# Forgetting attention inside a decoder block: one reduction over two neighbouring PSUM banks, query tiles in falling order, the causal mask written into the loaded row

## The chip, the cores and the metric

The kernel runs on one core of one Trainium2 chip. The metric is the device time of one execution in microseconds (us). The engines are TensorE (PE, matmul; PEld is its weight load), VectorE (DVE), ScalarE (ACT), GpSimd (POOL) and SyncE (SP, which issues most of the DMAs). An SBUF or PSUM tile has 128 partitions; a PSUM bank holds 512 fp32 values in each.

## The reference

One decoder block on 1024 tokens of width 1024. The part that matters here is forgetting attention: 8 heads of dimension 64, causal, with a decay that is summed up over the keys and subtracted from the logits, so that it acts as a row of 1024 numbers, one for each key, of each head.

```python
c = jnp.cumsum(log_f, axis=1)
logits = jnp.einsum('bqhd,bkhd->bhqk', qi, k).astype(jnp.float32) * scale
logits = logits + ci[..., None] - c_k
causal = pi[:, None] >= key_pos[None, :]
logits = jnp.where(causal, logits, -jnp.inf)
p = jax.nn.softmax(logits, axis=-1).astype(v.dtype)
return jnp.einsum('bhqk,bkhd->bqhd', p, v)
...
mix = jnp.concatenate([att, sg], axis=-1)
h = h + mix @ w_out[layer]
h = h + conv_ffn(rmsnorm(h, norm_ffn_g[layer]), w_up[layer], conv_w[layer], conv_b[layer], w_down[layer])
```

The other half of the width (`sg`) is a chunked spatial gating. Behind both stand the output projection, a norm, and a gated MLP with a short convolution.

## The kernel before

The kernel goes through stages: the input projections and the gating (to about 226 us in the trace), attention (226 to 391 us), the output projection with the second norm (to about 440), the up projection with the convolution (to about 858) and the down projection (to the end, 1075). Precision beyond that of the fast matmul comes from splitting an operand into a high and a low half, so that most products are made of two or three matmuls. In attention, ACT casts the high half and DVE computes the low one.

The order of instructions on each engine in attention is not written out by hand. The scheduler places them, with a few extra order edges (`after`). An engine carries out its own instructions in that order, so one that waits holds up everything behind it on its engine.

**One head (`att_head`, L752 to 831).** SP issues five loads: the queries `A` (L756), the keys `B` (L757), the head's row of decay sums, broadcast to all partitions, `ck` (L758), and the keys' other half `B2` in two pieces (L759, L760). `A` and `B` share a tile `x1`, `ck` and `B2` share a tile `x2`; each has two buffers, so that a head's loads can start when the head before the last has finished with the buffer. Then come four query tiles `i`, in the order 0, 1, 2, 3, each with two query blocks `j` = 2i and 2i+1 of 128 queries. Block `j` needs the first n = (j+1) x 128 keys. For each block:

- POOL copies the last one to four 128-column pieces of `ck` into the block's tile `t`, setting what the causal mask forbids to a large number (L776);
- PE computes the logits in one or two PSUM banks of 512 keys (tag `s`, four buffers), two matmuls each (L783, L784);
- DVE reduces each bank in one instruction (L786): the row is combined with the logits, written to `t`, and the minimum over the keys comes out. For blocks 4 to 7 there are two of these, and the second starts from the first one's minimum `mn`. In the trace each shows as two records, the reduction and the read of its accumulator;
- ACT takes the exponential of the whole block, with the minimum as bias (L789).

Then, for each pair of 128 keys, PE transposes the weights into a PSUM bank (L812), ACT casts the high half `pt` (L813), DVE computes the low half (L814), and PE multiplies with the values (L822; "PV" below). After an odd tile the two tiles' result in `po` is evacuated by ACT (L828) and DVE (L829).

**Around the heads.** `row_tail` (L724) turns the row sums of a finished head into reciprocals (DVE, L729), transposes them and sends them through DRAM back to 64 partitions (L734, L735). It stands in the tile 0 of the next head. `pair_end` (L738) scales and splits the result of two heads; it runs on POOL for the first three pairs (L744, L747, L750), in tile 2 of heads 2, 4 and 6, and on DVE for the last. `wo_load` copies and splits the output projection's weights on POOL (L873, L874): for the first two tiles they are ordered behind masks of head 5, for the other two behind the last of head 7.

**Fillers.** The gating half's share of the output projection (`sg_out`, L833 to 856) is cut into 16 units of 12 matmuls, which are handed out between query tiles by the list `FILLS`, one or two at a time: they stand in heads 0 to 2, and none is left from head 3 on.

**After attention.** The output projection's matmuls (`wmm`, L963 to 965) take four parts of the width, k = 0 to 3, each from one pair of heads. In the profile before, 17 of the 72 of k = 0 to 2 stand between the last matmuls of attention. The results are added to the residual at L973.

PSUM has eight banks: four with tag `b` (transposes, results, fillers) and four with tag `s` (logits), in the pool `psa`, which lives for the whole kernel.

Of the kernel before, what the change touches and what calls it, by code (L numbers as in the profile page):

```python
# [64 lines left out]
def block_kernel(ctx: ExitStack, tc: tile.TileContext, xT, xtok, wuv, wv, wqk, wf, cpk, bfv,  # L65
# [12 lines left out]
    psa = ctx.enter_context(tc.tile_pool(name="psa", bufs=4, space=bass.MemoryType.PSUM))  # L78
# [673 lines left out]
    def att_head(h, order=(0, 1, 2, 3)):  # L752
# [13 lines left out]
        for i in order:  # L766
# [3 lines left out]
            for jj in range(2):  # L770
# [4 lines left out]
                c0 = (j // 4) * 512  # L775
                sel = pool.affine_select(out=t[:, c0:n], in_=ck[:, c0:n], pattern=[[-1, n - c0]], compare_op=ALU.is_ge,  # L776
                                   fill=BIG, base=j * P - c0, channel_multiplier=1)
                mn = sml.tile([P, 2], F32, tag="mn", name=nm("mn"))
                lo_ = lim[:, 0:1]
                for c in range(0, n, 512):  # L780
                    e = min(n, c + 512)
                    ps = sbank()
                    pe.matmul(ps[:, 0:e - c], A[:, qs], B[:, c:e], start=True, stop=False)  # L783
                    pe.matmul(ps[:, 0:e - c], A[:, qs], B2[:, c:e], start=False, stop=True)  # L784
                    m = mn[:, c // 512:c // 512 + 1]
                    dve.tensor_tensor_reduce(out=t[:, c:e], in0=ps[:, 0:e - c], in1=(t if c == c0 else ck)[:, c:e], scale=1.0,  # L786
                                             scalar=lo_, op0=ALU.add, op1=ALU.min, accum_out=m)
                    lo_ = m
                ex = act.activation(t, t, AF.Exp, bias=lo_, scale=-1.0, accum_out=rs[:, j:j + 1])  # L789
                exs.append(ex)  # L790
            sels[h].append(sel)
            if h == 7 and i == 3:
                wo_load((2, 3))
                row_tail(7, None)
            if h > 0 and i == 0:
                row_tail(h - 1, ex)
            if h in (2, 4, 6) and i == 2:
                pair_end(p - 1, sel)
            for _ in range(FILL[4 * h + list(order).index(i)]):
                next(filler, None)  # L800
            if i % 2 == 0:
                po = bank()
# [21 lines left out]
            if i % 2 == 1:  # L824
# [65 lines left out]
    early.release()  # L890
    upl = tc.alloc_tile_pool(name="upl", bufs=1, reuse_waits="tile")
# [560 lines left out]
```

## Time and profile before

| | us |
|---|---|
| median of 3 runs | 1077.31 (1076.47 to 1077.58) |
| the profiled execution's own time | 1076.71 |
| its span in the trace | 1075.0 |
| attention, about 226 to 391 | 165 |
| in it: PE busy | 162.4 |
| in it: DVE busy | 122.9 |
| in it: ACT busy | 105.7 |
| in it: POOL busy | 59.5 |

The busy times of attention are those of the window from 226 to 391 us. In the rows of a timeline the first number is the start in us from the beginning of the span, the second the duration, then come engine, line, operation, what is written and what is read, the shape, and in brackets how long the engine sat idle before and what released it; "x2" joins two neighbours of one kind. A row of a grouped view gives, behind the bar, busy time in us and the mean duration in ns, then the idle time ahead of the group and its releasers.

### The profile page before, as it was taken

To read this page: it belongs to the slowest core of one execution; us is meant where nothing else is said; L and a number is where in the kernel's file an instruction comes from. 1 tells how busy PE (TensorE), PEld (TensorE's weight loads), DVE (VectorE), ACT (ScalarE), POOL (GpSimd) and SP (SyncE) were. 2 spreads that over 40 slices of the span, in tenths; PEclk is the share of its full clock that TensorE was granted. 3 is DMA by queue.
4 is the path that set the end of the run, shared out by engine and by line. 5 is a ranking of instruction groups with operands and counts; after the bars stand their busy time and mean duration, and the time that the engine had idled before them with its cause. 6 is when DMAs were issued, how large, how long until landed. Compare 5 with 4: busy or idle time off the path is not lost.

```text
span 1075.0 us, 14470 instructions
## 1 busy us (share of the span) xinstructions
PE 1062.7 (99%) x5013; PEld 876.6 (82%) x5013; DVE 892.4 (83%) x1363; ACT 568.0 (53%) x984; POOL 249.5 (23%) x223
## 2 busy tenths in 40 slices
PE   9999999999999999999999999999999999999997
PEld 7888788787888888878888888888888888888886
DVE  5985798775689969999899999989988776898774
ACT  6666644554468855764444444444444444454653
POOL 0002134233046541054333333333322000000000
PEclk9999999999999999999999999999999999999999
DMA  9242267937557445132244513222331899433442
GB/s 345 90 140 96 74 156 218 278 118 224 188 166 207 129 137 185 72 117 98 98 137 164 170 69 127 98 98 98 108 118 45 289 326 317 125 95 97 141 125 96
DMA packets 66297, 160.80 MB, mean 150 GB/s; under 512 B 7976, under 2 KB 8240, under 8 KB 66224
## 3 DMA queue, kind: packets, MB, share of 16 engines
q1 hardware_dynamic: 65792, 159.32, 45.4%
q8 instruction: 39, 0.64, 0.2%
q10 hardware_dynamic: 432, 0.57, 0.1%
q14 instruction: 34, 0.28, 0.1%
HBM read 117.06 MB, written 42.80 MB: 149 GB/s over the span
## 4 chain that ended last, share of the span: by engine, by line
PE 77%; ACT 2%; DVE 2%; issue 1%; POOL 0%; DMA 0%; DVEq 0%; ACTq 0%
PE k L1306 19%; PE qa L1054 11%; PE qc L1054 11%; PE qd L1054 11%; PE qb L1054 5%; PE pb L822 3%; PE pb L812 2%; PE ps L257 2%; PE pf L852 1%; PE pf L853 1%; PE pf L851 1%; PE ps L783 1%; PE ps L784 1%; PE pb L964 1%; PE pb L963 1%; PE pb L965 1%
## 5 line engine op out<-in xcount | busy, mean ns | idle before, releaser
L1306 PE MATMUL k<-whb,wha 128*128 128x512 f32 x924 | 209.7, 389 | 0.0
L1306 PEld LDWEIGHTS k<-whb,wha 128*128 128x128 f32 x924 | 173.3, 188 | 36.2 <-DVE wha L159 0.2
L1054 PE MATMUL qc<-xT,whb 128*128 128x512 f32 x540 | 129.8, 389 | 0.0
L1054 PE MATMUL qa<-xB,wha 128*128 128x512 f32 x528 | 127.2, 390 | 0.0
L1054 PEld LDWEIGHTS qc<-xT,whb 128*128 128x128 f32 x540 | 101.3, 188 | 21.2 <-ACT whb L153 0.2
L1054 PEld LDWEIGHTS qa<-xB,wha 128*128 128x128 f32 x528 | 98.8, 188 | 20.8 <-DVE wha L159 0.4
L153 ACT CAST wha<-sg 128x512 fp32r<-128x512 f32 x77 | 47.8, 622 | 96.9 <-PE k L1306 85.8
L153 ACT CAST whb<-sg 128x512 fp32r<-128x512 f32 x82 | 50.5, 617 | 86.6 <-PE qc L1054 67.0
L159 DVE TENSOR_TENSOR wha<-sg,wha 128x512 fp32r<-128x512 f32 x77 | 52.7, 687 | 41.1 <-ACT wha L153 41.0
L1054 PE MATMUL qd<-xB,whb 128*128 128x512 f32 x264 | 63.9, 389 | 0.5 <-DVE h L1173 0.5
L1054 PE MATMUL qd<-xT,whb 128*128 128x512 f32 x264 | 63.6, 389 | 0.0
L159 DVE TENSOR_TENSOR whb<-sg,whb 128x512 fp32r<-128x512 f32 x82 | 58.2, 710 | 4.4 <-ACT whb L153 4.3
L941 POOL TENSOR_TENSOR sg<-raw 128x512 f32<-128x512 f32 x20 | 30.7, 1535 | 134.0 <-DVE whb L159 75.7
L813 ACT CAST pt<-pb 128x512 fp32r<-128x512 f32 (+1 forms) x80 | 40.6, 543 | 38.5 <-PE pb L812 37.4
L1054 PE MATMUL qb<-xT,whb 128*128 128x512 f32 x252 | 60.9, 389 | 0.0
L822 PE MATMUL pb<-pt,V 128*128 128x256 f32 (+1 forms) x320 | 58.7, 298 | 1.6 <-ACT pt L813 1.2
L1054 PEld LDWEIGHTS qd<-xB,whb 128*128 128x128 f32 x264 | 49.5, 188 | 11.2 <-issue 0.9
L1054 PEld LDWEIGHTS qd<-xT,whb 128*128 128x128 f32 x264 | 49.6, 188 | 10.3
L822 PEld LDWEIGHTS pb<-pt,V 128*128 128x128 f32 x320 | 46.8, 188 | 13.5 <-ACT pt L813 8.9
L1054 PEld LDWEIGHTS qb<-xT,whb 128*128 128x128 f32 x252 | 47.3, 188 | 9.8
L814 DVE TENSOR_TENSOR pt<-pb,pt 128x512 fp32r<-128x512 f32 (+1 forms) x80 | 48.1, 632 | 8.0 <-ACT pt L813 7.4
L944 POOL TENSOR_TENSOR sg<-sg,raw 128x512 f32<-128x512 f32 x20 | 33.3, 1666 | 64.6 <-DVE whb L159 64.6
(399 smaller groups left out, 2306.9 us busy)
## 6 DMA issues: line engine op xcount, KB each, us to landing
raw<-wup SPq DMA_DIRECT2D x44, 512.0 KB, 3.5
sg<-hx SPq DMA_DIRECT2D x77, 256.0 KB, 2.8
hx<-hs SPq DMA_DIRECT2D x44, 256.0 KB, 3.7
hx<-ca SPq DMA_DIRECT2D x35, 256.0 KB, 2.0
xT<-wdn SPq DMA_DIRECT2D x28, 256.0 KB, 4.1
raw<-wqk SPq DMA_DIRECT2D x8, 512.0 KB, 4.7
qd<-G SPq DMA_DIRECT2D x16, 256.0 KB, 3.9
kd<-G SPq DMA_DIRECT2D x16, 256.0 KB, 3.3
```

The costliest lines, as they stand in the source:

```text
L153: act.copy(h, src)
L159: return eng.tensor_tensor(out=l, in0=src, in1=f32(h), op=ALU.subtract)
L257: pe.matmul(banks[m], xs(n, xi, k)[:, ms], w[:, wi, :], start=(first and k == 0 and c == 0), stop=(k == 3 and c == 2), skip_group_check=True)
L783: pe.matmul(ps[:, 0:e - c], A[:, qs], B[:, c:e], start=True, stop=False)
L812: pe.transpose(ptr[:, c:c + P], tj[jj][:, k * P:(k + 1) * P], ident)
L813: act.copy(pt[:, 0, 0:w], ptr[:, 0:w])
L814: dve.tensor_tensor(out=pt[:, 1, 0:w], in0=ptr[:, 0:w], in1=f32(pt[:, 0, 0:w]), op=ALU.subtract)
L822: pe.matmul(po[:, oo:oo + n], lhs, pt[:, s, o:o + n], start=(k == 0 and s == 0), stop=(s == 1 and half))
L941: pool.tensor_tensor(out=s[0], in0=a21, in1=a22, op=ALU.add)
L944: pool.tensor_tensor(out=s[3], in0=s[1], in1=a12, op=ALU.add)
L1054: pe.matmul(ps, w[:, wi, ks], xb[:, xi, k, :], start=(first and n == 0), stop=(n == 11), skip_group_check=True)
L1306: pe.matmul(banks[bk + m], xh[:, xi, ms], wh[:, wi, :], start=(first and p_ == 0 and n == 0), stop=(p_ == NP - 1 and n == 2), skip_group_c ...
```

## The change

The diff touches attention and the PSUM pools around it.

- The query tiles run in the order 3, 2, 1, 0, and in a tile the larger block first: blocks 7, 6, ... 0.
- The mask is no longer copied into `t`. POOL sets it in place in the loaded row `ck`, on the 128 columns of the diagonal alone. The block before in the order (j+1) has to have read those columns without the mask first, which the falling order gives.
- A block's logits lie in one tile of two neighbouring PSUM banks (tag `L`, two buffers), and DVE takes the whole block, up to 1024 columns, in one instruction. 96 reductions become 64.
- `ck` and `B2` lie in two tiles that are allocated once, with a half for each of an even and an odd head.
- What stood in tile 0 or tile 2 of a head (`row_tail`, `pair_end`) and the fillers go by the position in the order.
- The PSUM pool is released ahead of attention and again behind it, and taken anew, with waits by tile.

```diff
+    psa.release()
+    psa = tc.alloc_tile_pool(name="psb", bufs=4, space=bass.MemoryType.PSUM, reuse_waits="tile")
+
+    cks, b2s = sb("x2", [P, 2, 1024]), sb("x2", [P, 2, 1024], F32R)
+
+    def att_head(h, order=(3, 2, 1, 0)):
         p, hh = h // 2, h % 2
-        ab, nb = sb("x1", [P, 2, 1024], F32R), sb("x2", [P, 2, 1024], F32R)
-        A, B, ck, B2 = ab[:, 0, :], ab[:, 1, :], f32(nb[:, 0, :]), nb[:, 1, :]
+        ab = sb("x1", [P, 2, 1024], F32R)
+        A, B, ck, B2 = ab[:, 0, :], ab[:, 1, :], cks[:, hh, :], b2s[:, hh, :]
...
-        for i in order:
+        for pos, i in enumerate(order):
...
-            for jj in range(2):
+            for jj in (1, 0):
...
-                c0 = (j // 4) * 512
-                sel = pool.affine_select(out=t[:, c0:n], in_=ck[:, c0:n], pattern=[[-1, n - c0]], compare_op=ALU.is_ge,
-                                   fill=BIG, base=j * P - c0, channel_multiplier=1)
-                mn = sml.tile([P, 2], F32, tag="mn", name=nm("mn"))
-                lo_ = lim[:, 0:1]
+
+                sel = pool.affine_select(out=ck[:, qs], in_=ck[:, qs], pattern=[[-1, P]], compare_op=ALU.is_ge,
+                                         fill=BIG, base=0, channel_multiplier=1)
+                mn = sml.tile([P, 1], F32, tag="mn", name=nm("mn"))
+                ps = psa.tile([P, 1024], F32, tag="L", bufs=2, name=nm("pl"))
                 for c in range(0, n, 512):
                     e = min(n, c + 512)
-                    ps = sbank()
-                    pe.matmul(ps[:, 0:e - c], A[:, qs], B[:, c:e], start=True, stop=False)
-                    pe.matmul(ps[:, 0:e - c], A[:, qs], B2[:, c:e], start=False, stop=True)
-                    m = mn[:, c // 512:c // 512 + 1]
-                    dve.tensor_tensor_reduce(out=t[:, c:e], in0=ps[:, 0:e - c], in1=(t if c == c0 else ck)[:, c:e], scale=1.0,
-                                             scalar=lo_, op0=ALU.add, op1=ALU.min, accum_out=m)
-                    lo_ = m
-                ex = act.activation(t, t, AF.Exp, bias=lo_, scale=-1.0, accum_out=rs[:, j:j + 1])
+                    pe.matmul(ps[:, c:e], A[:, qs], B[:, c:e], start=True, stop=False)
+                    pe.matmul(ps[:, c:e], A[:, qs], B2[:, c:e], start=False, stop=True)
+                dve.tensor_tensor_reduce(out=t, in0=ps[:, 0:n], in1=ck[:, 0:n], scale=1.0,
+                                         scalar=lim[:, 0:1], op0=ALU.add, op1=ALU.min, accum_out=mn)
+                ex = act.activation(t, t, AF.Exp, bias=mn, scale=-1.0, accum_out=rs[:, j:j + 1])
                 exs.append(ex)
             sels[h].append(sel)
-            if h == 7 and i == 3:
+            if h == 7 and pos == 3:
                 wo_load((2, 3))
                 row_tail(7, None)
-            if h > 0 and i == 0:
+            if h > 0 and pos == 0:
                 row_tail(h - 1, ex)
-            if h in (2, 4, 6) and i == 2:
+            if h in (2, 4, 6) and pos == 2:
                 pair_end(p - 1, sel)
-            for _ in range(FILL[4 * h + list(order).index(i)]):
+            for _ in range(FILL[4 * h + pos]):
                 next(filler, None)
-            if i % 2 == 0:
+            if pos % 2 == 0:
                 po = bank()
...
-            if i % 2 == 1:
+            if pos % 2 == 1:
...
     early.release()
+    psa.release()
+    psa = tc.alloc_tile_pool(name="psc", bufs=4, space=bass.MemoryType.PSUM, reuse_waits="tile")
```

More of the change, by code (lines that the diff above doesn't have):

```diff
@@ L77, in block_kernel @@
     FTAG, FB, BB = FCFG
-    psa = ctx.enter_context(tc.tile_pool(name="psa", bufs=4, space=bass.MemoryType.PSUM))
+    psa = tc.alloc_tile_pool(name="psa", bufs=4, space=bass.MemoryType.PSUM)
     uid = [0]
@@ L1405, in block_kernel @@
     raws.release()
+    psa.release()
 def layouts(inp):
```

1 line of the change is left out of this document (removed).

## The prediction, made before the changed kernel had run

> **What bounds the kernel now.** I read the page first, for the engine that ends last over the whole span.
>
> ```profile
> span 1075.0 us, 14470 instructions
> PE 1062.7 (99%) x5013; PEld 876.6 (82%) x5013; DVE 892.4 (83%) x1363; ACT 568.0 (53%) x984; POOL 249.5 (23%) x223
> PE 77%; ACT 2%; DVE 2%; issue 1%; POOL 0%; DMA 0%; DVEq 0%; ACTq 0%
> ```
>
> TensorE sets the time of the program as a whole. A busy share of 99% does not say that every stage is full, because the ends of matmuls are modelled. The change touches attention alone, some 165 us, so that stage was cut into windows, with the busy time of each engine in each.
>
> ```profile
> core 0: us, PE busy (x) PEld busy (x) DVE busy (x) ACT busy (x) POOL busy (x), PEclk, DMA share, GB/s
> 226.00:250.00 24.00, 23.83 (x126) 19.56 (x125) 14.98 (x39) 11.10 (x24) 1.60 (x4) 1.00 0.40 138
> 290.00:310.00 20.00, 20.00 (x116) 16.79 (x115) 13.19 (x31) 8.32 (x18) 7.80 (x10) 1.00 0.21 71
> 310.00:330.00 20.00, 19.59 (x133) 16.89 (x133) 18.86 (x55) 17.63 (x43) 3.33 (x8) 1.00 0.93 288
> 330.00:350.00 20.00, 19.43 (x139) 17.18 (x139) 18.46 (x49) 16.73 (x39) 17.27 (x25) 1.00 0.59 172
> 350.00:370.00 20.00, 19.30 (x135) 17.01 (x134) 18.71 (x54) 16.46 (x37) 6.99 (x16) 1.00 0.55 172
> ```
>
> There are two regimes. Up to 310 us (heads 0 to 2) the filler matmuls keep PE full and DVE stands at 62 and 66% in the two windows shown: time saved on DVE there is worth nothing, and a DVE wait is covered as long as PE has fillers in front of what waits. From 310 to about 381 us (heads 3 to 7; their first and last reductions, in rows below, stand at 310.25 and 381.65, 14.3 us a head) DVE is busy 56.0 of 60 us, and PE is only kept looking busy. There the order on DVE is the pace. DVE's idle time is 4.0 us in those 60 us, 4.2 heads, or 0.95 us a head. The clock is 1.00 throughout, so no term comes from it. Next, what DVE's instructions take, one after the other.
>
> ```profile
> 310.25 0.35 DVE L786 CUSTOM_DVE_ANT_0 gg<-ps,gg,lim 128x128 f32<-128x128 f32 x1
> 310.52 0.08 DVE L786 DVE_READ_ACCUMULATOR2_ANT mn<- 128x1 f32 x1
> 310.52 0.48 DVE L786 CUSTOM_DVE_ANT_0 gg<-ps,gg,lim 128x256 f32<-128x256 f32 x1
> ...
> 316.16 0.56 DVE L814 TENSOR_TENSOR pt<-pb,pt 128x384 fp32r<-128x384 f32 x1 [0.20 <-ACT pt L813]
> 316.64 0.47 DVE L786 CUSTOM_DVE_ANT_0 H<-ps,H,mn 128x256 f32<-128x256 f32 x1
> ...
> 318.31 0.68 DVE L829 TENSOR_TENSOR H<-pb,H 64x512 f32<-64x512 f32 x1
> 318.99 0.69 DVE L814 TENSOR_TENSOR pt<-pb,pt 128x512 fp32r<-128x512 f32 x1
> 319.60 0.61 DVE L786 CUSTOM_DVE_ANT_0 H<-ps,H,mn 128x384 f32<-128x384 f32 x1
> 320.14 0.74 DVE L786 CUSTOM_DVE_ANT_0 H<-ps,x,lim 128x512 f32<-128x512 f32 x1
> 320.81 0.08 DVE L786 DVE_READ_ACCUMULATOR2_ANT mn<- 128x1 f32 x1
> ```
>
> The first column is the start, and from start to start counts what an instruction costs its queue: a reduction of 512 columns 0.67 (320.14 to 320.81), of 384 columns 0.54, of 128 columns 0.27 (310.25 to 310.52, the first reduction of head 3). That is 1.04 ns a column and 0.137 us fixed. The read of the accumulator starts before the reduction has ended and costs the queue nothing by itself. The low half L814 costs 0.61 (512) or 0.48 (384), the evacuation L829 0.68. By this an estimate for the new 1024-column reduction is 1.20, for 896 columns 1.07.
>
> **The change part by part.** *Merging.* 96 reductions become 64: in each head the four upper query blocks need one instead of two, which saves 4 x 0.137 = 0.55 us of queue. With it goes the second reduction's wait for the first one's minimum, where the two stand side by side.
>
> ```profile
> 380.65 0.08 DVE L786 DVE_READ_ACCUMULATOR2_ANT mn<- 128x1 f32 x1
> 380.90 0.75 DVE L786 CUSTOM_DVE_ANT_0 H<-ps,H,mn 128x512 f32<-128x512 f32 x1 [0.17 <-DVE mn L786]
> ```
>
> That is 0.17 to 0.25 us, in about one pair every second head: 0.1 a head. So -0.65 a head, -3.2 us for the five heads in which DVE is the pace. Bounds: 0 if the 1024 form costs as much as two of 512, and -5.8 if by busy time (512 against 128 columns, 0.74 against 0.34, is 0.21 fixed, with the 0.08 read 0.29; x 4 x 5). I take the start-to-start rate, since it is DVE's queue that sets the pace.
>
> *The mask in place.* Before, POOL copied the masked columns into a tile of its own, far ahead. Now the mask of block j-1 overwrites columns that the reduction of block j reads, so it cannot start before that reduction ends, and the next reduction waits for it: an exchange DVE, POOL, DVE. Its price comes from these rows of POOL and DVE.
>
> ```profile
> 330.96 0.65 POOL L776 TENSOR_SCALAR_AFFINE_SELECT gg<-x 128x128 f32<-128x128 f32 x2 [11.14 <-ACT t L789]
> 331.77 0.49 DVE L786 CUSTOM_DVE_ANT_0 t<-ps,t,mn 128x256 f32<-128x256 f32 x1 [0.17 <-POOL gg L776]
> ```
>
> A 128-column mask takes 0.33. The reduction's end lies 0.07 later than the point at which its queue would go on, and each of the two handovers costs between nothing and the 0.17 of the second row: 0.4 to 0.74. I take 0.5 us. It is exposed only where two reductions stand next to each other on DVE; the instruction order of the new kernel has two such places a head in heads 4 to 7 (blocks 6 and 5, blocks 4 and 3), the others have L814s between. 1.0 us a head, of which I let 0.45 fall into the 0.95 of idle time that DVE has now: +0.55 a head, +2.7 us. Bounds: 0, and +5 with nothing absorbed. Merging and exchanges thus nearly cancel.
>
> *The load of the decay row.* This is the largest term. The mask of the next head's block 7 needs that head's row in SBUF, and in POOL's order it now stands ahead of the current head's mask for block 5 (heads 4, 5 and 6; in head 3 ahead of block 4). The row's slot comes free only with the last reduction, block 0, of the head before. So POOL stands at the load, and behind it the current head's own masks, which DVE waits for, and then ACT and PE. Before, POOL waited for the same load, but its masks were so far ahead that nobody was late.
>
> ```profile
> 247.01 0.38 SPq L758 DMA_DIRECT2D x<-ncd  x1
> 309.46 0.32 SPq L758 DMA_DIRECT2D x<-ncd  x1
> 353.82 0.37 SPq L758 DMA_DIRECT2D x<-ncd  x1
> ```
>
> ```profile
> 252.45 0.65 POOL L776 TENSOR_SCALAR_AFFINE_SELECT gg<-x 128x128 f32<-128x128 f32 x2 [24.85 <-DMA x<-ncd]
> 316.49 0.65 POOL L776 TENSOR_SCALAR_AFFINE_SELECT gg<-x 128x128 f32<-128x128 f32 x2 [12.35 <-DMA x<-ncd]
> 359.81 0.65 POOL L776 TENSOR_SCALAR_AFFINE_SELECT gg<-x 128x128 f32<-128x128 f32 x2 [7.11 <-DMA x<-ncd]
> ```
>
> From SP's issue to POOL's start passed 5.4, 7.0 and 6.0 us. In the new kernel two masks (0.65) and handovers (0.2) follow, so block 5's reduction may start 6.3 to 7.9 us after block 0's ended; I take 6.9. DVE reaches it sooner: reciprocal 0.1, L829 0.68, L814 0.61, block 7 1.20, two L814 of 384 columns 0.96, block 6 1.07, together 4.6, with its present share of idle time about 5.1. Wait 1.8 us in each of three heads: +5.4; bounds 3 x 1.2 and 3 x 2.8, or nothing if SP issues sooner. In heads 1 to 3 the fillers hide it. [...]
>
> *POOL's blocks.* The heads' pair ends and the copies of the output weights used to run where the masks were long done. Now they stand in order between masks that DVE is waiting for.
>
> ```profile
> 332.60 1.17 POOL L873 CAST whl<-raw 128x512 fp32r<-128x512 f32 x2
> 333.73 2.53 POOL L874 TENSOR_TENSOR whl<-raw,whl 128x512 fp32r<-128x512 f32 x2
> 338.03 2.54 POOL L744 TENSOR_TENSOR H<-H 128x512 f32<-128x512 f32 x2 [1.77 <-DMA H<-rsd]
> 340.51 1.17 POOL L747 CAST A<-H 128x512 fp32r<-128x512 f32 x2
> 341.64 2.54 POOL L750 TENSOR_TENSOR A<-H,A 128x512 fp32r<-128x512 f32 x2
> ```
>
> A pair end is 6.25 us, one half of a weight tile 1.85. The pair end before head 7's block 6 starts after head 6's block-0 mask, and with the next mask makes 6.9 us from block 1's end; DVE has three L814 (1.70), block 0 (0.27) and 3.8 up to block 6, together 5.8: +1.0. The one before head 5's block 6 is swallowed by the longer wait for the row in that head (0). The one in head 2 stands between blocks 2 and 1, where DVE has 1.8 us of work: 4.5 late, of which fillers still queued on PE hide about half: +2 (0 to 4.5). Of the three weight halves in head 5, the one between blocks 4 and 3 shows: 1.85 + 0.33 against 1.4 of DVE work, +0.7. Together +3.7, bounds +1 to +7.
>
> *Start and end.* The heaviest tile now comes first.
>
> ```profile
> L789 ACT ACTIVATE t<-t,mn 128x1024 f32<-128x1024 f32 x4 | 4.6, 1154 | 2.1 <-DVE mn L786 2.1
> L789 ACT ACTIVATE gg<-gg,mn 128x128 f32<-128x128 f32 x8 | 3.2, 402 | 0.1
> ```
>
> Its first transposes come (1.28 + 1.15) - (0.34 + 0.40) = 1.7 us later than those of the lightest tile; fillers cover part: +1.0. At the end the lightest tile is last.
>
> ```profile
> 390.69 0.45 PE L822 MATMUL pb<-pt,V 128*128 128x256 f32 x3
> ...
> 393.08 0.39 PE L964 MATMUL pb<-whl,A 128*128 128x512 f32 x1
> 393.30 0.39 PE L965 MATMUL pb<-whl,A 128*128 128x512 f32 x1
> ```
>
> Before, 9.5 us pass from the last reduction's end (381.65) to the last PV's (391.14), with 17 of the 72 first output matmuls already done by then: 55 x 0.2275 = 12.5 remain, together 22.0. After, none of the 72 stands earlier: 4.7 us for the last light tile (my estimate from the L814 and L813 rates) and 16.4, together 21.1. I take -0.7 (-2 to +1).
>
> *Sum.* -3.2 + 2.7 + 5.4 + 3.7 + 1.0 - 0.7 = +8.9. What remains of DVE's idle time, 0.5 us a head or 2.5 in five heads, can take up later waits: +6.4. The profiled execution took 1076.71, so 1083.1; the median of the runs lies 0.6 above it: 1083.7. The two output tiles of 1024 columns instead of four banks I cost at nothing: the next logits wait for the reduction two before, and 4 x 0.2275 of matmuls fit under the one reduction between (0.94 to 1.20 us). Stages after attention run in the same order on all engines and only shift.
>
> **The rivals.** *Paced by DVE alone, and faster.* If SP, POOL and the handovers stay ahead, the exchanges and the load cost nothing, and only merging and the end remain: -3.9, or -6.5 by the busy rate: 1073 us, at the lowest 1071. For it speaks that DVE is busy 93% while POOL is mostly idle; against it, that the row's slot is freed by block 0 and the load's rows are longer than DVE's work. It decides where block 5's mask is done within 5.1 us of block 0. *The load is hidden, the rest holds.* Then 6.4 - 5.4 = +1.0: 1078.3, no difference that can be told. For it, one issue-to-use of 5.4; against it, the longer two. [...] *Everything through POOL.* If DVE meets each of the seven exchanges of a head with no work in hand, that is 17.5 instead of 2.7, the load at its upper bound is 8.4 and the blocks 7: with the other terms some +30, less 2.5 that idle time takes: about 1104. Against it, the L814s that stand between. *The 1024 form is no cheaper than two of 512.* Then +3.2 on the forecast: 1086.9; the straight line from 128 to 512 columns speaks against it.
>
> **How the numbers follow.** Forecast with the dear form among it: 0.59, own range 1077.5 to 1091. Faster by DVE's pace 0.22; load hidden 0.11; everything through POOL 0.08. From 1072 to 1092 I leave out the last rival and the lowest part of the first. A measurement of this kernel tells about 0.2% (2.2 us) from no change: faster 0.22, same 0.14 (most of the hidden load, the lower edge of the forecast), slower 0.64.
>
> **What would show it.** Right: in heads 4 to 6 DVE idle 1 to 3 us ahead of block 5's reduction, released by POOL, and POOL idle ahead of it by the row's load; gaps of 0.3 to 0.5 us between the reductions of blocks 6 and 5, and 4 and 3; the 1024-column reduction at about 1.28 us busy; and the stages after 440 us unchanged in length. Wrong: loose heads shorter than 14.3 us; POOL waiting for the load and DVE not; a late part elsewhere, in the weights' loads or in the PSUM pools' handover to the output stage.

## The result: 2.5% slower, and the profile after

The changed kernel takes 1105.4 us (median; 1102.1 to 1106.3) against 1077.4 before: a ratio of 1.0252, 95% interval 1.0235 to 1.0268. The prediction had 1083.7 with a range up to 1092: the sign was right, 28 us stand against the 6.4 that were summed up. One more execution, the one profiled with the result, ran below the full clock from beginning to end (0.70 of it in the mean), took 1420.6 us and is left out; the profile shown here is of another execution of the same kernel, 1104.0 us by itself with a span of 1102.3. In its rows the mask is L782, the logits are L788 and L789, the reduction is L790, the transposes L815, the low half L817, PV L825, the row's load L764, the pair end L744 to L750 as before, the copies of the output weights L876 and L877.

The page of the changed kernel:

```profile
span 1102.3 us, 14400 instructions
PE 1073.8 (97%) x5013; PEld 883.0 (80%) x5013; DVE 890.9 (81%) x1299; ACT 570.9 (52%) x984; POOL 242.5 (22%) x223
PE 67%; issue 9%; DVE 3%; POOL 3%; ACT 1%; DMA 0%; SPq 0%; POOLq 0%; ACTq 0%; DVEq 0%
```

DVE and POOL do less work than before (DVE 890.9 against 892.4, POOL 242.5 against 249.5), and the span is 27.3 us longer. In the chain that ended last, PE's share fell from 77 to 67%. The up projection starts at 464.7 us instead of 437.4, 27.3 later, and lasts as long as before: all of the loss lies ahead of it, 26.2 of it before the last reduction. The windows of attention (length, then busy time of PE, PEld, DVE, ACT and POOL, PE's granted clock, DMA share and GB/s):

```profile
290.00:310.00 20.00, 20.00 (x113) 15.95 (x112) 12.61 (x22) 9.13 (x18) 1.46 (x5) 1.00 0.39 122
310.00:330.00 20.00, 16.63 (x95) 13.74 (x93) 12.83 (x30) 12.06 (x28) 8.62 (x15) 0.91 0.60 168
330.00:350.00 20.00, 16.43 (x104) 14.29 (x103) 14.31 (x32) 13.71 (x32) 2.59 (x9) 0.91 0.66 189
350.00:370.00 20.00, 16.92 (x102) 14.90 (x102) 13.44 (x30) 13.09 (x29) 13.83 (x20) 0.83 0.40 119
370.00:390.00 20.00, 18.21 (x118) 15.52 (x116) 14.07 (x32) 14.61 (x33) 5.53 (x12) 0.91 0.54 171
```

Two things are new against the windows of before. No engine is full: DVE stands at 12.8 to 14.3 of 20 us where it was at 18.5 to 18.9, PE at 16.4 to 18.2. And the granted clock is below 1. The view of waits of the same kernel between 226 and 412 us says who waits for whom (total us, times, longest):

```profile
POOL x L782 <- DVE mn L790: 108.3, 50, 9.4
...
POOL x L782 <- DMA x<-ncd: 21.2, 5, 7.7
PEld pl L788 <- DVE mn L790: 16.8, 19, 2.8
...
PE pl L788 <- DVE mn L790: 9.4, 12, 2.7
...
DVE t L790 <- POOL x L782: 4.4, 4, 2.4
DVE gg L790 <- POOL x L782: 3.8, 3, 3.0
DVE wy L790 <- POOL x L782: 3.6, 7, 1.2
...
DVE H L790 <- POOL x L782: 3.4, 3, 2.6
```

POOL's wait for DVE costs nothing by itself: POOL has nothing else to do. But DVE waits 15.2 us for POOL's masks (4.4 + 3.8 + 3.6 + 3.4; 0.2 before), and PE's logits wait for DVE's reductions (9.4 us on PE, 16.8 on its weight loads, which overlap; 0.2 and 0.9 before). DVE's 15.2 us are 17 stops: twelve exchanges of 0.40 us each, three waits behind the row's load (2.43, 2.58 and 1.18) and two behind other work of POOL (3.03 in head 2, 1.17 in head 5). The chain of one such stop, in head 5, in the timeline of POOL, DVE and PE:

```profile
357.23 0.30 POOL L782 TENSOR_SCALAR_AFFINE_SELECT x<-x 128x128 f32<-128x128 f32 x1 [0.47 <-DVE mn L790]
357.48 0.61 POOL L876 CAST whl<-raw 128x512 fp32r<-128x512 f32 x1
358.18 1.28 POOL L877 TENSOR_TENSOR whl<-raw,whl 128x512 fp32r<-128x512 f32 x1
361.17 0.54 POOL L782 TENSOR_SCALAR_AFFINE_SELECT x<-x 128x128 f32<-128x128 f32 x2 [1.71 <-DMA x<-ncd]
...
358.01 1.14 DVE L790 CUSTOM_DVE_ANT_0 H<-pl,x,lim 128x896 f32<-128x896 f32 x1
...
361.74 1.02 DVE L790 CUSTOM_DVE_ANT_0 H<-pl,x,lim 128x768 f32<-128x768 f32 x1 [2.58 <-POOL x L782]
...
359.85 0.27 PE L789 MATMUL pl<-x,x 128*128 128x128 f32 x1
362.82 0.79 PE L788 MATMUL pl<-x 128*128 128x512 f32 x1 [2.70 <-DVE mn L790]
```

POOL waits for the next head's row until 361.17, then sets two masks: the next head's first and, behind it, this head's block 5. DVE has nothing to do in between (2.58 us), and PE, whose next logits need the two-bank tile that block 5's reduction frees, stands for 2.70 us. This is the stop that the prediction described, at the place that it named. What follows it was not in the prediction: the first matmul behind the gap, of 512 columns, takes 0.79 us, where those of the kernel before take 0.43 in the mean (L783).

How long the heads are, in us, from a head's first reduction to that of the next (the last to the end of the last reduction):

| head | 0 | 1 | 2 | 3 | 4 | 5 | 6 | 7 | all |
|---|---|---|---|---|---|---|---|---|---|
| before | 27.5 | 32.8 | 23.4 | 12.4 | 17.4 | 15.3 | 12.6 | 13.7 | 155.0 |
| changed | 23.5 | 40.5 | 29.2 | 15.8 | 19.6 | 20.1 | 18.1 | 13.8 | 180.6 |
| changed, POOL's order mended (e12) | 23.6 | 40.6 | 25.4 | 15.6 | 16.4 | 16.5 | 17.1 | 14.0 | 169.1 |

### The profile page after: what moved, and what is told of

The parts are those of the page before. It is cut to its first block, busy times and chain, and to the rows that moved or that the text cites. A ratio compares the mean times of both kernels' runs of the same rounds, so it can differ in the third digit from the quotient of the medians.

```text
span 1418.9 us, 14400 instructions
## 1 busy us (share of the span) xinstructions
PE 1404.1 (99%) x5013; PEld 971.7 (68%) x5013; DVE 880.1 (62%) x1299; ACT 578.6 (41%) x984; POOL 227.9 (16%) x223
## 4 chain that ended last, share of the span: by engine, by line
PE 89%; issue 7%; POOL 2%; DVE 1%; ACT 0%; DMA 0%; SPq 0%; POOLq 0%; ACTq 0%; DVEq 0%
PE k L1311 18%; PE qc L1059 11%; PE qa L1059 11%; PE qd L1059 11%; PE ps L257 6%; PE pb L257 6%; PE qb L1059 5%; PE qd L401 2%; PE qa L401 2%; PE qc L401 2%; PE pb L825 2%; PE pb L815 2%; PE qb L401 1%; PE pb L968 1%; PE pb L969 1%
## 5 line engine op out<-in xcount | busy, mean ns | idle before, releaser
L1311 PE MATMUL k<-whb,wha 128*128 128x512 f32 x924 | 262.3, 456 | 0.0
L1311 PEld LDWEIGHTS k<-whb,wha 128*128 128x128 f32 x924 | 183.5, 199 | 78.7
L1059 PE MATMUL qc<-xT,whb 128*128 128x512 f32 x540 | 166.7, 469 | 0.0
L1059 PE MATMUL qa<-xB,wha 128*128 128x512 f32 x528 | 163.3, 470 | 0.0
L1059 PEld LDWEIGHTS qc<-xT,whb 128*128 128x128 f32 x540 | 108.6, 201 | 50.4 <-issue 5.3
L1059 PE MATMUL qd<-xT,whb 128*128 128x512 f32 x264 | 81.5, 467 | 0.0
L1059 PE MATMUL qd<-xB,whb 128*128 128x512 f32 x264 | 81.3, 466 | 0.0
L1059 PE MATMUL qb<-xT,whb 128*128 128x512 f32 x252 | 77.5, 466 | 0.0
L825 PE MATMUL pb<-pt,V 128*128 128x256 f32 (+1 forms) x320 | 67.1, 340 | 1.7 <-ACT pt L816 1.4
L825 PEld LDWEIGHTS pb<-pt,V 128*128 128x128 f32 x320 | 57.9, 224 | 11.6 <-ACT pt L816 4.6
L817 DVE TENSOR_TENSOR pt<-pb,pt 128x512 fp32r<-128x512 f32 (+1 forms) x80 | 49.1, 635 | 19.0 <-ACT pt L816 18.4
```

Source lines behind the costliest of these rows:

```text
L817: dve.tensor_tensor(out=pt[:, 1, 0:w], in0=ptr[:, 0:w], in1=f32(pt[:, 0, 0:w]), op=ALU.subtract)
L825: pe.matmul(po[:, oo:oo + n], lhs, pt[:, s, o:o + n], start=(k == 0 and s == 0), stop=(s == 1 and half))
L1059: pe.matmul(ps, w[:, wi, ks], xb[:, xi, k, :], start=(first and n == 0), stop=(n == 11), skip_group_check=True)
L1311: pe.matmul(banks[bk + m], xh[:, xi, ms], wh[:, wi, :], start=(first and p_ == 0 and n == 0), stop=(p_ == NP - 1 and n == 2), skip_group_c ...
```

## The clock of TensorE falls to half behind a gap

The granted clock was followed through the changed kernel in steps of 3.41 us, because its falls lay at multiples of that from each other (317.11, 344.42, 361.48 and 381.96 us: 8, 5 and 6 steps). Columns as above; the clock is the number right behind POOL:

```profile
313.70:317.11 3.41, 1.04 (x8) 0.66 (x6) 0.38 (x2) 0.58 (x1) 3.20 (x4) 1.00 0.71 204
317.11:320.52 3.41, 3.03 (x10) 2.64 (x11) 1.93 (x8) 1.37 (x5) 0.29 (x1) 0.51 0.78 284
320.52:323.94 3.42, 3.22 (x20) 2.49 (x20) 3.20 (x6) 2.53 (x5) 0.48 (x2) 0.99 0.96 231
...
341.00:344.42 3.42, 1.18 (x6) 0.79 (x6) 2.40 (x4) 1.64 (x4) 0.83 (x3) 1.00 0.74 172
344.42:347.83 3.41, 3.15 (x13) 3.16 (x14) 2.52 (x8) 1.87 (x5) 0.88 (x3) 0.51 0.28 77
...
358.07:361.48 3.41, 1.82 (x12) 1.39 (x11) 1.09 (x3) 2.24 (x6) 1.62 (x4) 1.00 0.85 187
361.48:364.90 3.42, 2.08 (x7) 1.80 (x8) 2.42 (x5) 1.42 (x3) 2.21 (x4) 0.51 0.01 4
364.90:368.31 3.41, 3.41 (x16) 3.29 (x16) 2.78 (x7) 2.41 (x6) 2.46 (x5) 0.50 0.22 77
...
378.55:381.96 3.41, 1.89 (x11) 1.38 (x11) 2.20 (x5) 2.42 (x6) 0.83 (x3) 1.00 1.05 232
381.96:385.38 3.42, 3.42 (x15) 2.94 (x14) 2.99 (x8) 2.08 (x6) 0.58 (x2) 0.51 0.54 213
...
405.86:409.27 3.41, 2.52 (x18) 2.14 (x18) 2.44 (x7) 2.25 (x6) 3.41 (x5) 1.00 0.00 0
```

A step in which PE was busy 1.04, 1.18, 1.82 or 1.89 us at full clock is followed by a step at half clock (0.50 or 0.51); so is one of 2.08 us that ran at half clock itself. A step with 2.52 us is not (405.86; the clock stays 1.00 behind it). In four of the five half-clock steps PE is busy for 3.0 to 3.4 us with 10 to 16 matmuls, where most steps at full clock hold 20 to 30. The five last 17.1 us, and PE is busy in 15.1 of them; by an estimate from the granted 0.50, full clock would need half of that for the same work, so they cost PE 7.5 us at most. Before there was no such step in attention (1.00 in every window). PE's longest wait in this stage of the changed kernel is 2.70 us.

How busy a step must be is not settled by these runs. Two steps of other runs, in the same columns:

```profile
350.23:353.64 3.41, 2.41 (x8) 1.19 (x8) 3.23 (x10) 2.87 (x6) 3.41 (x9) 1.00 0.00 0
...
395.31:398.72 3.41, 1.62 (x13) 1.36 (x14) 0.22 (x2) 3.38 (x7) 0.00 (x0) 1.00 0.12 38
```

The first is of e1, and the step behind it runs at 0.50; the second is of e8, and behind it the clock stays at 1.00. So a fall came behind a step that was busy for 2.41 us and none behind one of 1.62: busy time as the profile models it doesn't tell where the clock falls.

The spread of the runs themselves agrees with a cost of about one for one. The changed kernel took 1102.1 us in the run with a mean clock of 0.994 and 1106.3 in the one with 0.990: 4.2 us more, and 0.004 of its span is 4.4 us. Over 37 runs in eight sets (the changed kernel twice, e1, e2, e3, e6, e9, e11), each run taken against the mean of its set, a microsecond of span lost to the clock (span times one minus the mean clock, known to 1.1 us) goes with 0.97 us of time, at a correlation of 0.76.

## The experiments

All times are medians, and ratios stand against the kernel before on the same chip, with their 95% intervals.

**e0: the changed kernel again.** No edit.

> The changed kernel once more, for an undisturbed profile. Theory (exchanges DVE-POOL-DVE, the wait for the decay row and POOL's blocks stretch attention): about 1105 us, attention (165 us before) longer by 20 us or more, DVE idle ahead of its reductions with POOL as releaser, and the stages behind it as long as before. Rival (the loss is the clock, since the runs' mean granted clock is 0.991 against 0.998): attention longer by less than 20 us, and stages after it longer than before at a granted clock below 1.

1105.5 us. The profile above is this one. Both readings held in part: attention is longer by more than 20 us and the stages behind it are as long as before, which the rival did not expect, but the clock is a part of the loss inside attention.

**e1: falling order alone.**

```diff
-    def att_head(h, order=(0, 1, 2, 3)):
+    def att_head(h, order=(3, 2, 1, 0)):
...
-        for i in order:
+        for pos, i in enumerate(order):
...
-            for jj in range(2):
+            for jj in (1, 0):
```

(with `pos` for `i` in the conditions, as in the change).

> The kernel before with the query tiles in falling order and nothing else. Theory: the order by itself costs little, 1075 to 1081 us. Rival (the heavy tile first, with its row sums and pair ends at other places, is what costs): 1090 us or more.

1090.0 us, 1.0107 (1.0090 to 1.0124): the rival. The falling order costs 12.2 us with four single banks, 96 reductions and copied masks. Its timeline shows one of two like places, at the turn to head 5:

```profile
343.20 2.53 POOL L744 TENSOR_TENSOR H<-H 128x512 f32<-128x512 f32 x2 [7.83 <-DVE rs L729]
345.68 1.17 POOL L747 CAST A<-H 128x512 fp32r<-128x512 f32 x2
346.81 2.52 POOL L750 TENSOR_TENSOR A<-H,A 128x512 fp32r<-128x512 f32 x2
349.28 1.69 POOL L776 TENSOR_SCALAR_AFFINE_SELECT H<-x 128x512 f32<-128x512 f32 x4
...
349.93 0.75 DVE L786 CUSTOM_DVE_ANT_0 H<-ps,H,mn 128x512 f32<-128x512 f32 x1 [2.89 <-POOL H L776]
...
350.74 0.39 PE L783 MATMUL ps<-x 128*128 128x256 f32 x1 [1.90 <-DVE mn L786]
```

The pair end stands in front of the masks of the next head. DVE is late by 2.89 us, PE by 1.90, and from 353.6 on PE runs 3.4 us at half clock (0.50). The same happens at 386 us: there PE is late by 2.08.

**e2: the mask copied, the rest of the change kept.**

```diff
-                sel = pool.affine_select(out=ck[:, qs], in_=ck[:, qs], pattern=[[-1, P]], compare_op=ALU.is_ge,
-                                         fill=BIG, base=0, channel_multiplier=1)
+                sel = pool.affine_select(out=t, in_=ck[:, 0:n], pattern=[[-1, n]], compare_op=ALU.is_ge,
+                                         fill=BIG, base=j * P, channel_multiplier=1)
...
-                dve.tensor_tensor_reduce(out=t, in0=ps[:, 0:n], in1=ck[:, 0:n], scale=1.0,
+                dve.tensor_tensor_reduce(out=t, in0=ps[:, 0:n], in1=t, scale=1.0,
```

> The changed kernel with the mask copied into the block's own tile again (all n columns of it, since the one reduction takes one operand), falling order and merged reductions kept. Theory: no exchange and no mask behind a reduction, so POOL runs ahead again; most of the loss is gone, 1073 to 1081 us. Rivals (falling order, or two logits tiles of two banks instead of four banks): 1095 us or more.

1102.8 us, 1.0232 (1.0217 to 1.0247): the theory fell. But POOL doesn't run ahead here either. A pair end and the copies of the output weights stand in front of the first masks of heads 5 and 7, which are now up to 1024 columns long, and the first reductions of these heads wait for them:

```profile
352.57 1.28 DVE L790 CUSTOM_DVE_ANT_0 H<-pl,H,lim 128x1024 f32<-128x1024 f32 x1 [3.44 <-POOL H L782]
...
390.27 1.28 DVE L790 CUSTOM_DVE_ANT_0 H<-pl,H,lim 128x1024 f32<-128x1024 f32 x1 [4.92 <-POOL H L782]
```

PE stands for 3.13 and 4.64 us behind them, and 13.7 us of attention run at half clock (17.1 in the changed kernel). So the 2.7 us between the two kernels are the mask in place less what the copies cost; the run doesn't give either price alone.

**e3: a head's first mask behind the last of the head before.**

```diff
+                if h > 0 and j == 7:
+                    after(tc, sel, sels[h - 1][3])
```

> The changed kernel with one order edge more: the first mask of a head stands behind the last mask of the head before, so that POOL no longer stands at the next head's decay row while this head's masks wait. Theory of the prediction (that wait is the largest term): 5 to 8 us faster than the changed kernel, 1097 to 1100 us. If the exchanges carry the loss: within 3 us of the changed kernel's 1105.

1099.7 us, 1.0198 (1.0181 to 1.0216), 5.8 below the changed kernel: near what the prediction put on this wait (5.4), and far from all. Not all of the 5.8 is that wait. The reductions of block 5 in heads 4 to 6 wait for POOL 1.8 us instead of 6.2, but the pair ends now stop the first masks of heads 5 and 7 (1.33 and 1.66 us), so that DVE's whole wait for POOL only falls from 15.2 to 13.4 us; and the profile has 10.2 us at half clock in attention instead of 17.1.

**e4: merged reductions and two logits tiles in rising order, mask copied.**

```diff
-    def att_head(h, order=(3, 2, 1, 0)):
+    def att_head(h, order=(0, 1, 2, 3)):
...
-            for jj in (1, 0):
+            for jj in (0, 1):
```

(on top of e2).

> Rising order as before, mask copied into the block's tile (all n columns), but one reduction over two neighbouring banks and two logits tiles, with the released and renewed PSUM pools. Theory A (falling order is what makes PE wait for reductions; merging alone saves DVE 0.55 us a head): 1073 to 1078 us. Theory B (two logits tiles instead of four banks make PE's next logits wait for a long reduction, in any order): 1085 us or more, with PE idle released by the reduction, and windows at half clock.

1090.4 us, 1.0120 (1.0105 to 1.0135): theory B in time. But the wait that it named is small, 0.5 us on PE's logits and 2.9 on their weight loads (0.2 and 0.9 before), and the half-clock steps that it expected are missing (none in attention).

**e5: the PSUM pool released and renewed, nothing else.**

```diff
-    psa = ctx.enter_context(tc.tile_pool(name="psa", bufs=4, space=bass.MemoryType.PSUM))
+    psa = tc.alloc_tile_pool(name="psa", bufs=4, space=bass.MemoryType.PSUM)
...
+    psa.release()
+    psa = tc.alloc_tile_pool(name="psb", bufs=4, space=bass.MemoryType.PSUM, reuse_waits="tile")
...
     early.release()
+    psa.release()
+    psa = tc.alloc_tile_pool(name="psc", bufs=4, space=bass.MemoryType.PSUM, reuse_waits="tile")
```

> The kernel before, with the PSUM pool released and taken anew ahead of attention and behind it, nothing else. Both theories: within 1.5 us of before. If the pools' handover costs (a wait for all banks at the two borders): 1080 us or more.

1083.1 us, 1.0054 (1.0039 to 1.0069): 5.6 us slower. Heads 3 to 7 are as long as before, to 0.1 us. The last reduction ends 2.8 us later (head 0 takes 29.7 instead of 27.5), and from there to the up projection another 3.2 are lost. The timeline of PE at the end of attention shows why:

```profile
393.03 0.56 PE L825 MATMUL pb<-pt,V 128*128 128x256 f32 x3 [0.20 <-DVE pt L817]
393.42 0.45 PE L968 MATMUL pb<-whl,A 128*128 128x512 f32 x1
```

The first matmul of the output projection comes after the last PV. Before, 17 of them stood between attention's last matmuls, from 379.5 us on. At the other end the first head's logits stood among the matmuls of the gating, from 217.7 us on, and now come after them, from 225.3. A released pool is a wall in the scheduler's order.

**e6: fillers spread in the changed kernel.**

```diff
-FILLS = [1, 2] * 10 + [2] + [0] * 11
+FILLS = [1, 0] * 12 + [1] * 4 + [0] * 4
```

> The changed kernel with the 16 filler units spread over heads 0 to 6 (one in every second tile, the last four in head 6) instead of heads 0 to 2. If the loss is PE standing idle and then running at half clock in heads 3 to 7, fillers in the gaps win back most of it: 1085 us or less, and fewer than two windows at half clock in attention. If the chain DVE-POOL-DVE is the pace whatever PE does, heads 3 to 6 stay as long as they are (16 to 20 us) and only heads 0 to 2 shorten: still faster, but PE idle before the logits stays at 10 us or more.

1095.9 us, 1.0173 (1.0156 to 1.0190), 9.5 below the changed kernel. Neither reading held: the time is above the 1085 of the first, and heads 3 to 6 did not stay as long as they were. Ten units went into these heads, 120 matmuls of 0.227 us or 27.2 us, and the heads are 18.3 us longer (91.9 against 73.6), so the fillers do cover part of the gaps. What remains is mainly one stop: PE's logits wait 7.5 us for reductions (9.4 in the changed kernel), and 6.1 of that lie at one place in head 7, where POOL copies output weights ahead of a mask, no filler is left, and three half-clock steps follow one another.

**e7: the same spread in the kernel before.** The same edit of `FILLS`.

> The kernel before with the same spread of the fillers. Its late heads are paced by DVE (93% busy) with PE matmuls to spare, its early ones by PE: 1065 to 1075 us if the two can be evened out; if the extra DVE work of a filler (0.69 us each) in the late heads takes the gain back, within 3 us of 1077.

1072.7 us, 0.9956 (0.9942 to 0.9971): faster than both kernels. But not as expected. DVE's first reductions of heads 1 and 6:

```profile
242.18 0.34 DVE L786 CUSTOM_DVE_ANT_0 gg<-ps,gg,lim 128x128 f32<-128x128 f32 x1
...
340.80 0.34 DVE L786 CUSTOM_DVE_ANT_0 gg<-ps,gg,lim 128x128 f32<-128x128 f32 x1
```

Five heads with two units each take 19.7 us a head. Without fillers a late head took 14.3, and two units are 24 matmuls of 0.227, or 5.4: the fillers lengthen a head by their full time on PE, where their work on DVE is only two additions of 0.69 us. The last reduction ends at 381.1, as before (381.65); of the 3.4 us that this profile is shorter, 2.7 were won between there and the up projection.

**e8: two logits tiles alone.** On e5, in rising order, with all 96 reductions and the masks as before:

```diff
+                pl = psa.tile([P, 1024], F32, tag="L", bufs=2, name=nm("pl"))
                 for c in range(0, n, 512):
                     e = min(n, c + 512)
-                    ps = sbank()
+                    ps = pl[:, c:c + 512]
```

> The kernel before with the renewed pools (1083.1 us by itself) and the logits in two tiles of two neighbouring banks instead of four single banks; rising order, masks and all 96 reductions as before. Theory (two tiles hold two blocks where four banks held up to four, so PE's look-ahead shrinks): 1087 to 1092 us, most of what rising order with merged reductions lost (1090.4). Rival (the merged instruction or the full-width mask copies cost it): within 2 us of 1083.

1092.0 us, 1.0143 (1.0125 to 1.0161): the two tiles by themselves cost 8.9 us over e5, and merging on top of them (e4, with longer mask copies and with the row and `B2` allocated once) wins 1.6 back. The windows of heads 3 to 7 in e5 and then in e8, and two rows of e8 at a head's turn, in which the two engines wait for each other:

```profile
313.06:384.48 71.42, 69.16 (x479) 60.46 (x477) 66.86 (x183) 60.69 (x142) 38.88 (x60) 1.00 0.58 181
...
313.30:395.25 81.95, 78.28 (x505) 63.39 (x503) 69.76 (x187) 62.38 (x145) 40.03 (x60) 1.00 0.56 168
...
350.48 0.75 DVE L790 CUSTOM_DVE_ANT_0 H<-pl,x,lim 128x512 f32<-128x512 f32 x1 [1.01 <-PE pl L788]
...
351.30 0.33 PE L787 MATMUL pl<-x 128*128 128x128 f32 x1 [0.27 <-DVE mn L790]
```

A block of at most 512 keys used to hold one bank of four and now holds a whole tile of two: PE can be two blocks ahead where it was up to four. The waits are short (0.2 to 1.0 us), many, and go both ways: in attention DVE's reductions wait 6.0 us for logits in 15 places (e5: 1.3 in 4), and the weight loads of the logits wait 7.2 us for reductions in 19 (e5: 0.3 in one). DVE's wait for ACT's casts ahead of the low half grows with them, from 7.2 us in e5 to 11.2. By the windows DVE sits idle for 12.2 us of heads 3 to 7 in e8 and for 4.6 in e5, ACT for 19.6 and 10.7: nearly the same instructions take longer, and all engines wait more.

**e9: PE kept busy in the gaps.** 12 matmuls of 384 columns, whose results nobody reads, added to the logits of block 4 in heads 4 to 6, with order edges that keep them between the two halves of these logits:

```diff
+                    dms = []
+                    if h in (4, 5, 6) and j == 4 and c == 512:
+                        dms = [pe.matmul(ps[:, 640:1024], A[:, 0:P], B[:, 0:384], start=True, stop=True) for _ in range(12)]
+                        after(tc, dms[0], m1)
+                    m0 = pe.matmul(ps[:, c:e], A[:, qs], B[:, c:e], start=True, stop=False)
+                    if dms:
+                        after(tc, m0, dms[-1])
```

> The changed kernel with 12 matmuls of 384 columns (some 2 us) whose results nobody reads, in the logits of block 4 of heads 4, 5 and 6, where PE otherwise stands idle 1.3 to 2.7 us for POOL's late masks. The waits for POOL stay. If the half-clock windows behind these gaps cost time of their own (up to 1.7 us each, four of them in those heads): 3 to 7 us faster than the changed kernel, 1098 to 1102 us, and fewer half-clock windows. If PE's clock is no part of the pace there: 1105 to 1111 us.

1112.6 us, 1.0333 (1.0315 to 1.0351): 7 us slower. The half-clock step behind head 4's gap at 341 us is gone, but the instructions around the new ones stand in another order, and attention still has 13.7 us at half clock (17.1 in the changed kernel), some at places where that one had none. This run doesn't tell the two readings apart.

**e10: falling order alone, pair ends one head later.** On e1:

```diff
-            if h in (2, 4, 6) and pos == 2:
+            if h in (3, 5, 7) and pos == 1:
                 pair_end(p - 1, sel)
```

> Falling order alone (1090.0 us), with each pair end on POOL put one head on (second tile of the next odd head instead of third tile of the even one), so that it no longer stands ahead of the masks of blocks 7 to 4 of heads 5 and 7. If those two stops (DVE idle 2.9 and 3.1 us, then PE idle 1.9 and 2.1 and 3.4 us at half clock each) are what falling order costs late: 1081 to 1085 us. If the order of the tiles itself costs it: 1088 us or more.

1082.5 us, 1.0051 (1.0033 to 1.0069): 7.5 below e1 (6.8 when each is taken against the kernel before on its own chip), and no half-clock step in attention. The two gaps of PE in e1 were 1.90 and 2.08 us, and its two half-clock steps cost 3.4 at most: together 7.4. The falling order keeps 5.4 us of its own: 2.7 in heads 0 to 2 and 3.4 in heads 3 to 7 in the profile, less a little at the end.

**e11: another spread of the fillers.**

```diff
+FILLS = [1, 1, 1, 0] * 2 + [1, 1, 0, 0] * 5 + [0] * 4
```

> The kernel before with the fillers spread another way (three units in each of heads 0 and 1, two in each of heads 2 to 6, on neighbouring tiles). A filler in a late head lengthened it by its full PE time (2.7 us), so attention as a whole should not shorten; what the first spread won came at attention's end. Same gain expected: 1070 to 1075 us; if that gain hung on the four units in head 6: 1077.

1077.4 us, 0.9999 (0.9983 to 1.0015), with runs from 1074.2 at a mean clock of 0.999 to 1081.4 at 0.995: the gain of e7 hangs on where its units stand, and 4.3 of the 7.1 us between these two runs are the clock's (0.004 of the span).

**e12: POOL's order mended in the changed kernel.** On e3; `pair_steps` is `pair_end` given out one instruction at a time:

```diff
+                if pend[0] is not None:
+                    after(tc, sel, pend[0])
+                    pend[0] = None
+                if h in (3, 5, 7) and j == 5:
+                    steps[0] = pair_steps(p - 1)
+                if j <= 5:
+                    st = next(steps[0], None)
+                    if st is not None:
+                        after(tc, st, sel)
+                        pend[0] = st
...
-            if h in (2, 4, 6) and pos == 2:
-                pair_end(p - 1, sel)
...
-                after(tc, pool.tensor_copy(w[hf][:, 0], src), sels[5][2 * k + hf] if k < 2 else sels[7][3])
+                after(tc, pool.tensor_copy(w[hf][:, 0], src), sels[6][2 * k + hf] if k < 2 else sels[7][3])
```

> The changed kernel with POOL's order mended throughout: a head's first mask behind the last of the head before, a pair end taken one instruction at a time between the masks of the next odd head, the weight copies one at a time between the masks of head 6. If POOL's order (load, pair ends, weight copies) and the half-clock windows that its gaps bring are what lies between the changed kernel (1105 us) and the sum of the renewed pools and two logits tiles (about 1091): 1089 to 1094 us, at most one half-clock window. If the exchanges with POOL, one a block, carry it: 1097 us or more, with DVE idle ahead of its reductions still 10 us or more.

1092.5 us, 1.0143 (1.0126 to 1.0160): 12.9 below the changed kernel, and no half-clock step in attention. Its waits:

```profile
PEld pl L811 <- DVE mn L813: 10.3, 20, 1.0
...
PE pl L811 <- DVE mn L813: 5.3, 14, 0.7
...
DVE wy L813 <- POOL x L793: 3.3, 7, 0.9
...
DVE t L813 <- POOL x L793: 1.8, 4, 0.6
...
DVE H L813 <- POOL x L793: 1.2, 3, 0.4
...
DVE gg L813 <- POOL x L793: 0.8, 2, 0.4
```

DVE's wait for POOL is 7.1 us in 16 places (15.2 in 17), none above 0.93. These are the exchanges: 14 of the 16 are 0.40 us. What remains above before, 15.1 us, stands beside 13 to 15 us that the renewed pools and the two tiles cost without any falling order (e4, e8).

## Why the prediction was wrong, point by point

**How the 28 us divide.** The renewed pools cost 5.6 (e5), two logits tiles 8.9 on top (e8), merging with full-width copies -1.6 (e4 against e8), the falling order 12.2 (e1), the mask in place 2.7 (the changed kernel against e2). These are differences between relatives and need not add up. That they do, 27.8, and for e2 25.1 where 25.0 were measured, is in part luck: 7.5 of the falling order's 12.2 hung on where the pair ends stand (e10), and e2 has stops and half-clock steps that e1 doesn't have. The sounder division goes through POOL: its order with the half-clock steps that it brought is 12.9 (e12), and the 15.1 that remain are about what the pools and the two tiles cost in rising order (12.9 in e4, 14.9 in e8).

**"There the order on DVE is the pace" failed.** It was read from DVE busy 56.0 of 60 us, with PE, at 58.3 of the same 60, "only kept looking busy". The runs say otherwise: fillers added to those heads cost their full PE time (e7), and 32 reductions fewer won 1.6 us (e4 against e8; e4's mask copies are longer, but none of its reductions waits for one). PE isn't simply full either, by an estimate: a late head has matmuls of 18432 columns in all, 8.2 us at 0.2275 for 512, and 36 transposes that start 0.11 us apart, 4.0, together 12.2 of its 14.3 us. A loop through PE, DVE and ACT, in which time added to PE counts and time taken from DVE mostly doesn't, would fit this and e8, where all engines wait more for nearly the same instructions; no run shows it by itself. So the first term, -3.2, had the right price for the instruction (1.19 us from start to start for 1024 columns, 355.88 to 357.07, against 1.20 forecast) and twice the worth that was measured.

**"The two output tiles I cost at nothing" failed, for 8.9 us.** The argument compared one reduction with four matmuls, as if the logits were PE's only work. With two tiles the logits wait for reductions and the reductions for logits, and the transposes, casts and low halves behind them come later too (the waits under e8). That a logits matmul which stands for a tile holds back all that is behind it on PE is the likely way; it was not followed through the queue.

**The pools' handover was not priced, for 5.6 us.** The prediction saw that no output matmul stands between attention's last ones any more, and set this against the light last tile in one term (-0.7; measured from the last reduction to the first residual sum at L973, 23.0 before and 22.6 after). That term came out nearly right; but its own list of what would show it wrong names this handover without a price: the same wall stands at attention's start, and without the light tile behind it (e5) the end alone lost 3 us.

**"The clock is 1.00 throughout, so no term comes from it" failed, for up to 7.5 us of PE's time in the profile.** The clock of before holds for the gaps of before. The change made four gaps of 1.3 to 2.7 us on PE, and behind them stand five half-clock steps of up to 1.7 us each.

**The load of the decay row was right as a wait.** Forecast +5.4 in three waits of 1.8 us; DVE waited 2.43, 2.58 and 1.18 us in heads 4 to 6, together 6.2. That e3 won nearly the same, 5.8, is partly luck: it saved 4.4 of these waits, brought others, and had 6.8 us less at half clock, which the term did not hold. POOL started 7.6, 7.7 and 6.3 us after SP's issue, two of them above the 5.4 to 7.0 of before.

**POOL's blocks were about right as waits and had no clock term.** +3.7 was forecast. The one in head 2, forecast at 2, kept DVE idle for 3.0 us up to 317, and PE stood there for 2.4 us (by the profile until the queries' load), with a half-clock step behind it; the weight copy in head 5, forecast at 0.7, cost 1.17; the pair end in head 7, forecast at 1.0, nothing. Together that is 4.2. From e3 to e12 the time falls by 7.2: DVE's waits for POOL by 6.4, and the time at half clock from 10.2 us to none.

**The exchanges had the right size; what they cost in time is open.** The forecast took 0.5 us for one, exposed in two places a head, and let part of it vanish: +2.7. Each takes 0.40 us of DVE's time, and heads 3 to 7 of e12 have two apiece. That kernel lies 2.1 us above e4, which has no exchanges and rising order, but they were not priced by themselves.

**Start and end**, +0.3 for the falling order, missed it: apart from POOL's blocks it costs 5.4 us (e10, with four single banks). Where these go wasn't followed further; the weight loads of the logits wait 3.8 us for reductions there (0.9 before).

**The rivals.** "Everything through POOL" had the right time, 1104, by the wrong sum: 17.5 of its microseconds were seven exposed exchanges a head, and DVE's whole wait for POOL, loads and blocks included, was 15.2. "Paced by DVE alone" fell with the premise that it shares with the forecast. The signs that the prediction set for being right all came true (the waits ahead of block 5, gaps of 0.40 us, 1.28 us for the long reduction, later stages as long as before), and yet its sum held 6.4 of 28 us: they showed that its mechanism was there, not that it was all.

## What to carry to other kernels

Before counting what an instruction saves on a busy engine, ask what happens if work is added or taken away there: an engine that is 93% busy need not be the pace, and a filler moved into the stage (e7) tells it at once. Buffers between two engines are a price of their own: a two-bank tile halves how many small blocks the producer can be ahead (8.9 us in e8), and a released pool stops the scheduler from mixing two stages (5.6 us in e5). Where a change can open gaps on PE, price each with the half-clock step that can follow it (here 3.41 us long, up to 1.7 us of PE's time), and look at what stands ahead of a small but urgent instruction on its engine (here POOL's masks behind a load, a pair end, a weight copy).

## What the runs showed that was not expected

In the changed kernel PE's clock fell to half (0.50) for 3.41 us after each step of the same length in which PE was busy 1.9 us or less, with no wait of PE longer than 2.7 us, and stayed at 1.00 after one with 2.5 us; but in e1 it fell after 2.41 us, and in e8 it stayed after 1.62. The mean clock differs from execution to execution, and with it the same program spreads by several us: 1074.2 at 0.999 to 1081.4 at 0.995 in e11. And the kernel before is beaten by another list of fillers: 1072.7 us with them spread (e7).
